# Splitting the weights of the output projection and the feed-forward ahead, as a background stream, and storing the parts through GpSimd's DMA queue

## The chip, the cores and the metric

The kernel runs on one core of a Trainium2 chip. The metric is the time of one execution on the device, in microseconds. A core has five engines, each of which works through its own instructions in order: PE (matrix multiply, with PEld for loading its weights), DVE (vector), ACT (scalar), POOL (GpSimd) and SP (here it only issues DMAs). A DMA is issued by an engine's queue, and an issue that has to wait for a semaphore holds up everything behind it on that engine. In what follows SPq is SP's queue.

## The reference, cut to what matters

One layer of a hybrid encoder for 2048 prompt frames with 16 meta tokens ahead, and 64 sample frames. Rows go through an RMS norm and one wide projection, whose columns feed three groups of mixers; their outputs go through the output projection and a gated feed-forward.

```python
def _trunk(x, states, segs, p):                       # DEPTH = 1
    m, ns = _mixer(_rmsnorm(x, p['norm1_w'][l]), ...)
    x = x + m
    x = x + _swiglu(_rmsnorm(x, p['norm2_w'][l]), p['w_gate'][l], p['w_up'][l], p['w_down'][l])
    return _rmsnorm(x, p['final_norm_w']), ...

def _mixer(h, ...):
    proj = einsum('btd,dn->btn', h, p['w_in'][l])     # 1024 x 5384
    ...                                               # Mamba-2 SSD, RWKV-7, HGRN2
    out = einsum('btm,md->btd', y, p['w_out'][l])     # 1536 x 1024

def _swiglu(h, wg, wu, wd):                           # 1024 x 2816, twice, and 2816 x 1024
    return (silu(h @ wg) * (h @ wu)) @ wd
```

All inputs are float32. The three mixers are causal and carry a state, so frames go through them in order.

## The kernel before, in words

**Tiles.** Rows are cut into 17 tiles (tile 0: the 64 sample frames and the 16 meta tokens; tiles 1 to 16: 128 prompt frames each). The projection (`projection`) works on three blocks of rows, each of two chunks of three tiles (`BLOCKS`, `CHUNKS`). Its results go to DRAM scratch. The mixers read them back a tile at a time: `rw_mixer` (RWKV) is one stream of work, `hs_mixer` (HGRN and SSD) a second. The output projection and feed-forward (class `Ffn`: `out`, `ffn`, `down`, `rest`) work on five groups of tiles: three of three tiles (`EARLY`), then two of four (`LATE`).

**Weights in two parts.** Every float32 weight is multiplied as two parts, hi (rounded) and lo (the rest), and every row operand too, so that a product takes three matmuls. Weights come in units of 128x512. `load_unit` (L205 to 221) gives a unit's two parts in one tile `w` of the ring, of which there are WB = 5. The first time a unit is used, it is loaded as float32 into a tile `raw` (L215, of which there are RB = 3), ACT rounds it into the hi half of `w` (L216), POOL (three units of four) or DVE (the fourth) subtracts to give the lo half (L218), and SP stores the whole `w` of 512 KB to DRAM (L220). Each later use of that unit is one load of 512 KB (L212). There are 84 units of the input projection, and 156 units of the output projection (24), gate and up (88) and down (44).

So the 84 units are split in block 0 of the projection, while PE uses them, and the 156 units in the first pass of the output projection and feed-forward (tiles 0 to 2, `fs[0]`), while PE uses them.

**Streams.** `flow` runs the main work (first the projection, then the early groups). Each piece of it yields its cost, which moves a clock `now` on; a `Stream` whose own clock `t` is not beyond `now` gets the next piece of its work put into the program, and its clock moves on by that piece's cost times the stream's scale (RWX, HSX). So the mixers are written into the program between the matmuls of the main work. A scheduler that knows estimated durations then sets the order on each engine; where a tile of a ring is used again, the instruction that writes it waits until the former use has ended. `drain` steps all streams until given tiles have gone through the mixers.

**DMA queues.** Almost all DMAs are issued by SP. POOL issues the mixers' results (`y`, L750, L879, L972), the final states and part of the output.

Of the kernel before, what the change touches and what calls it, by code (L numbers as in the profile page):

```python
# [9 lines left out]
F32 = mybir.dt.float32  # L10
# [9 lines left out]
P = 128  # L20
# [19 lines left out]
CF = 2  # L40
GKS = 1
GLO = 3
URB = 6
RWX, HSX, HSD = 1.05, 1.0, 6.0
COL = 1 / 2360
AHEAD = 4
KOUT = [8, 9, 10, 11, 0, 1, 2, 3, 4, 5, 6, 7]
# [29 lines left out]
def body(tc, A, O, blocks=None, supers=None, dbg=None):  # L77
# [14 lines left out]
    def mk(p, shape, dt=F32, tag=None, bufs=None):  # L92
        uid[0] += 1
        kw = {} if bufs is None else {"bufs": bufs}
        return p.tile(list(shape), dt, tag=tag, name=f"{tag}_{uid[0]}", **kw)
# [110 lines left out]
    def load_unit(src):  # L206

        key = str(src)
        wt = mk(ring, [P, 2, 512], F32, tag="w", bufs=WB)
        hi, lo = wt[:, 0].bitcast(F32R), wt[:, 1].bitcast(F32R)  # L210
        if key in split:
            nc.sync.dma_start(wt, split[key])  # L212
            return hi, lo
        raw = mk(ring, [P, 512], tag="raw", bufs=RB)
        nc.sync.dma_start(raw, src)  # L215
        S.activation(hi, raw, AF.Copy)  # L216
        units[0] += 1
        (G if units[0] % 4 < GLO else V).tensor_tensor(lo, raw, wt[:, 0], SUB)  # L218
        d = split[key] = dram.tile([P, 2, 512], F32, tag=f"w{units[0]}", name=f"w{units[0]}")
        nc.sync.dma_start(d, wt)  # L220
        return hi, lo

    def inv_rms(p, ss, n, w, mult, eps):
        V.tensor_scalar(ss[:n], ss[:n], mult, eps, MUL, ADD)  # L224
# [840 lines left out]
    nc.sync.dma_start(Shg, A["hg_s0"])  # L1065
    nc.sync.dma_start(Sss, A["ss_s0"])

    def projection():
        for si, sb in enumerate(sbs):
            tiles = sum([CHUNKS[ci] for ci in sb], [])  # L1070

            head = (lambda ci: chunk[ci].v()) if si else (lambda ci: g1([ci], "rw", A["w_rw"], range(HEAD)))
            yield from head(sb[0])
            for ci in sb[1:]:
                if si == 0:
                    chunk[ci].fetch()
                yield from chunk[ci].load()
                yield from head(ci)
            yield from g1(sb, "rw", A["w_rw"], range(0 if si else HEAD, 14))
            ready["rw"] += tiles  # L1080
            banks = yield from gemm_dt(A["w_dt"], [(chunk[ci].hT, chunk[ci].N) for ci in sb])
            dts = [chunk[ci].dt(ps) for ci, ps in zip(sb, banks)]

            def after(ct):
                if ct in DSTEP:
                    for d in dts:
                        next(d, None)
            after(-1)
            yield from g1(sb, "hg", A["w_hg"], range(12), after)
            yield from g1(sb, "xb", A["w_xb"], range(8))  # L1090
            nxt = sbs[si + 1] if si + 1 < len(sbs) else []
            if nxt:
                chunk[nxt[0]].fetch()
            if si == 0:
                for ci in sb:
                    yield from chunk[ci].v()
            for i, ci in enumerate(sb):
                tail = chunk[ci].z()
                yield from weave(tail, chunk[nxt[0]].load()) if nxt and i else tail
            if nxt:  # L1100
                for ci in nxt[1:]:
                    chunk[ci].fetch()
            ready["hs"] += tiles
            if si == 0:
                nc.sync.dma_start(O["s_shift"], scarry)
                nc.sync.dma_start(O["s_conv"], sccarry)
            if si == len(sbs) - 1:
                nc.sync.dma_start(O["p_shift"], carry)
                nc.sync.dma_start(O["p_conv"], ccarry)
# [328 lines left out]
```

## Time and profile before

| what | value |
|---|---|
| median of 3 runs | 3614.21 us (3605.3 to 3619.85) |
| profiled execution, its own time | 3607.34 us |
| its span in the profile | 3605.6 us, 60375 instructions |
| PE / PEld busy | 96% / 84% of the span |
| DVE / ACT / POOL busy | 54% / 30% / 17% of the span |
| mean granted PE clock | 0.982 |
| moved by DMA | 825.75 MB, 229 GB/s over the span |

The stages, from the span's start, in us: block 0 of the projection to about 400, blocks 1 and 2 to 1389, then the first pass of output projection and feed-forward to 1874, the second to 2322, the third (its last part beside group 3's output projection), and from 2618 on the last groups, with no mixers left. Busy is the time in which an engine has an instruction under way. For PE it is a poor measure of the work done, since a matmul that takes longer at a lower granted clock is busy all the same.

### The profile page before, as it was taken

Reading aid. Unit: us, or ns where it says so; the run is one execution under the profiler, and the core shown is the slowest. Engines: PE = TensorE matmul, PEld = TensorE weight load, DVE = VectorE, ACT = ScalarE, POOL = GpSimd, SP = SyncE. Lnnn points to the kernel's source line nnn. Section 1 sums busy time; section 2 is a strip of 40 time slices with the busy share of each in tenths; the row PEclk is TensorE's granted clock in tenths of the full one; section 3 lists DMA queues with packets and bytes.
Section 4 is the critical chain, followed back from the end, with each engine's and each line's share of the span. In section 5 each row is a group of like instructions: output and inputs, shape, how many; then the busy total and the mean of one; then the engine's idle time right before and its main releaser. Section 6 shows DMA issues by size and latency. Waiting matters only on the chain.

```text
span 3605.6 us, 60375 instructions
## 1 busy us (share of the span) xinstructions
PE 3462.9 (96%) x23056; PEld 3033.5 (84%) x23056; DVE 1960.2 (54%) x4612; ACT 1067.1 (30%) x2380; POOL 610.1 (17%) x811
## 2 busy tenths in 40 slices
PE   7999999999999998989889999999999999999998
PEld 7998689989799996778778988879989888878887
DVE  3358546558756676787776676666423322232223
ACT  4445333344433444434343122331110101010001
POOL 3325202102111123345431010110000000000000
PEclk9999999999999999899999999999999999999999
DMA  8776865555666668788897776766867755556554
GB/s 308 233 228 219 291 209 177 159 171 176 239 213 183 198 205 303 263 282 311 299 312 258 229 226 228 249 227 220 287 218 245 263 191 188 181 204 208 193 194 170
DMA packets 396106, 825.75 MB, mean 229 GB/s; under 512 B 107985, under 2 KB 195545, under 8 KB 393769
## 3 DMA queue, kind: packets, MB, share of 16 engines
q1 hardware_dynamic: 389912, 802.75, 67.1%
q0 software_dynamic: 5904, 19.14, 1.4%
q8 instruction: 182, 2.98, 0.3%
q14 instruction: 108, 0.88, 0.1%
HBM read 617.71 MB, written 204.04 MB: 228 GB/s over the span
## 4 chain that ended last, share of the span: by engine, by line
PE 43%; DMA 6%; DVE 6%; SPq 1%; issue 1%; POOL 1%; ACT 1%; DVEq 0%; POOLq 0%; ACTq 0%
PE g L106 32%; PE d L106 6%; PE c L106 2%; PE h L106 2%; DMA w<-w 1%; DMA raw<-in_w_down 1%; DMA raw<-in_w_up 1%; DVE acc L1264 0%; DMA b4k<-psc 0%; DMA y<-hin 0%; DVE Xp L637 0%; DMA hin<-hg 0%; DVE tp L636 0%; POOL w L218 0%; DMA psc<-L 0%
## 5 line engine op out<-in xcount | busy, mean ns | idle before, releaser
L106 PE MATMUL g<-h2hi,w 128*128 128x384 f32 (+2 forms) x3520 | 986.1, 357 | 12.9 <-DMA w<-w 4.6
L106 PE MATMUL g<-hhi,w 128*128 128x384 f32 (+3 forms) x3312 | 835.5, 330 | 11.6 <-DMA w<-w 4.4
L106 PEld LDWEIGHTS g<-h2hi,w 128*128 128x128 f32 x3520 | 639.2, 189 | 81.9 <-ACT w L216 6.9
L106 PE MATMUL g<-h2lo,w 128*128 128x384 f32 (+2 forms) x1760 | 625.4, 355 | 0.0
L106 PEld LDWEIGHTS g<-hhi,w 128*128 128x128 f32 (+1 forms) x3312 | 581.6, 188 | 26.7 <-POOL w L218 4.1
L106 PE MATMUL g<-hlo,w 128*128 128x384 f32 (+3 forms) x1680 | 550.7, 328 | 0.0
L106 PEld LDWEIGHTS g<-h2lo,w 128*128 128x128 f32 x1760 | 332.3, 189 | 32.7 <-DVE h2lo L251 0.2
L106 PEld LDWEIGHTS g<-hlo,w 128*128 128x128 f32 (+1 forms) x1680 | 314.8, 187 | 5.7
L218 POOL TENSOR_TENSOR w<-raw,w 128x512 fp32r<-128x512 f32 x180 | 247.8, 1379 | 336.6 <-ACT w L216 292.4
L106 PE MATMUL g<-w,mhi 128*128 128x512 f32 x792 | 264.0, 410 | 13.0 <-ACT w L216 4.4
L1222 DVE TENSOR_TENSOR w2k<-g,w2k 128x512 f32<-128x512 f32 x44 | 30.4, 692 | 363.1 <-PE g L106 357.0
L226 POOL TENSOR_TENSOR rs<-ss,half 128x1 f32<-128x1 f32 (+2 forms) x51 | 31.0, 609 | 1132.8 <-DVE ss L224 1119.8
L106 PE MATMUL d<-w,mhi 128*128 128x512 f32 x704 | 216.7, 389 | 0.0
L216 ACT ACTIVATE w<-raw 128x512 fp32r<-128x512 f32 x240 | 149.5, 627 | 197.0 <-PE g L106 52.0
L106 PEld LDWEIGHTS g<-w,mhi 128*128 128x128 f32 x792 | 148.9, 193 | 49.4 <-ACT w L216 5.9
L106 PE MATMUL g<-w,hhi 128*128 128x512 f32 (+1 forms) x544 | 179.2, 410 | 10.9 <-DMA w<-w 7.0
L1264 DVE TENSOR_TENSOR acc<-d,acc 128x512 f32<-128x512 f32 x176 | 121.6, 692 | 119.6 <-PE d L106 118.2
L106 PE MATMUL g<-w,h2hi 128*128 128x512 f32 x544 | 175.8, 402 | 10.4 <-DMA w<-w 6.8
L636 DVE TENSOR_TENSOR tp<-Xp,b4k 128x60 f32<-128x60 f32 (+24 forms) x527 | 132.1, 251 | 66.6 <-DMA b4k<-psc 54.0
L106 PE MATMUL g<-w,mlo 128*128 128x512 f32 x396 | 158.6, 401 | 0.0
L106 PEld LDWEIGHTS d<-w,mhi 128*128 128x128 f32 x704 | 132.2, 188 | 27.9
L1264 DVE TENSOR_TENSOR acc<-g,acc 128x512 f32<-128x512 f32 (+1 forms) x198 | 132.4, 683 | 41.1 <-PE g L106 41.0
(359 smaller groups left out, 5299.5 us busy)
## 6 DMA issues: line engine op xcount, KB each, us to landing
w<-w SPq DMA_DIRECT2D x1088, 512.0 KB, 4.1
hin<-hg SPq DMA_DIRECT2D x16, 1280.0 KB, 6.2
rin<-rw SPq DMA_DIRECT2D x16, 896.0 KB, 6.1
yr<-y SPq DMA_DIRECT2D x51, 256.0 KB, 4.7
hg<-stage SPq DMA_DIRECT2D x64, 192.0 KB, 3.0
sin<-ss SPq DMA_DIRECT2D x16, 768.0 KB, 6.1
raw<-in_w_gate SPq DMA_DIRECT2D x44, 256.0 KB, 4.3
raw<-in_w_up SPq DMA_DIRECT2D x44, 256.0 KB, 4.3
```

Source lines behind the costliest of these rows:

```text
L106: return T.matmul(out, lhsT, rhs, start=start, stop=stop)
L216: S.activation(hi, raw, AF.Copy)
L218: (G if units[0] % 4 < GLO else V).tensor_tensor(lo, raw, wt[:, 0], SUB)
L226: G.tensor_tensor(rs[:n], ss[:n], half[:n, 0:w], ALU.pow)
L636: V.tensor_tensor(tv, _bc(Xp[:, 0:m, q], 2, w), _bc(Up[:, q, q + 1:32], 1, m), MUL)
L1222: V.tensor_tensor(sg[:, NS], pu[:, NS], sg[:, NS], MUL)
L1264: V.tensor_tensor(self.acc[:n, i, cs], ps[:n], self.acc[:n, i, cs], ADD)
```

## The change

**A fourth stream.** After block 0 of the projection a third stream beside the two mixers is started, `split_ahead(later())`. `later` lists the sources of all 156 later units in the order of their first use. For each source `split_ahead` loads it into a tile `raw` (SP), ACT rounds it into a second tile of the same ring, POOL subtracts in place (`raw` becomes the lo part), and POOL issues two stores of 256 KB each, one of the hi and one of the lo part, to the unit's place in DRAM. Each unit counts as cost 1.0, and the scale is SPX = 5.0, so a unit is put into the program at every 5 units of `now`. Where `load_unit` later finds the source in `split`, it only loads the 512 KB. The ring `raw` still has three tiles, of which a unit of the stream takes two. DVE has no part in these units.

**The other queue.** The store in `load_unit` (block 0's units) is issued by POOL in place of SP.

```diff
+SPX = 5.0
...
-        nc.sync.dma_start(d, wt)
+        G.dma_start(d, wt)
         return hi, lo
+
+    def split_ahead(srcs):
+
+        for src in srcs:
+            if str(src) in split:
+                continue
+            raw, hi = (mk(ring, [P, 512], tag="raw", bufs=RB) for _ in range(2))
+            nc.sync.dma_start(raw, src)
+            S.activation(hi.bitcast(F32R), raw, AF.Copy)
+            G.tensor_tensor(raw.bitcast(F32R), raw, hi, SUB)
+            units[0] += 1
+            d = split[str(src)] = dram.tile([P, 2, 512], F32, tag=f"w{units[0]}", name=f"w{units[0]}")
+            for i, part in enumerate((hi, raw)):
+                G.dma_start(d[:, i], part)
+            yield 1.0
...
+    def later():
+
+        yield from (A["w_out"][hf, k] for hf in range(2) for k in KOUT)
+        for f in range(NFF):
+            yield from (A[n][f][:, k0 * P:(k0 + 4) * P] for n in ("w_gate", "w_up") for k0 in range(0, KD, 4))
+            if f % CF == CF - 1:
+                yield from (A["w_down"][g * P:(g + 1) * P, hf * 512:hf * 512 + 512]
+                            for hf in range(2) for g in range(f + 1 - CF, f + 1))
...
             if si == 0:
+                streams.append(Stream(split_ahead(later()), SPX))
                 nc.sync.dma_start(O["s_shift"], scarry)
```

**What moves in the order.** The scheduler's order was read for both kernels; a line number of the changed kernel is 1 higher in `load_unit` and 16 higher behind the new function `split_ahead`. Three places matter.

On SP, in the first pass of the feed-forward (gate and up of tiles 0 to 2). Before, each unit is a load of `raw` and, in between, the store of an earlier unit:

```order
L215 DMA raw_18323<-in_w_gate 128x512
L220 DMA w_18262<-w_18257 128x1024
L215 DMA raw_18352<-in_w_gate 128x512
L220 DMA w_18269<-w_18264 128x1024
L215 DMA raw_18377<-in_w_up 128x512
L220 DMA w_18327<-w_18322 128x1024
L215 DMA raw_18426<-in_w_up 128x512
L220 DMA w_18356<-w_18351 128x1024
```

In the changed kernel the units of that pass are loads of both parts (L213), and the stream's last sources (L230) stand between them:

```order
L213 DMA w_17980<-w_10003 128x1024
L230 DMA raw_19473<-in_w_gate 128x512
L213 DMA w_18003<-w_10137 128x1024
L213 DMA w_18017<-w_10207 128x1024
L213 DMA w_18052<-w_10321 128x1024
L213 DMA w_18074<-w_10461 128x1024
L213 DMA w_18097<-w_10554 128x1024
L230 DMA raw_19538<-in_w_up 128x512
```

No store is left on SP there. Of the stream's 156 units, 131 stand on ACT ahead of the first operation of that pass, and the other 25 in it.

On POOL, in a later block of the projection, around an update of the RWKV state (`Srw`; `carry` and `graw` belong to the projection's epilogue, `us` to the HGRN mixer). Before:

```order
L687 TENSOR_TENSOR Srw_6935<-Srw_5583,pc_6219 128x512
L348 COPY carry<-graw_6481 128x1
L346 COPY graw_6489<-carry 128x1
L346 COPY graw_6603<-carry 128x1
L348 COPY carry<-graw_6489 128x1
L782 TENSOR_TENSOR us_6514<-us_6513,us_6514 128x256
```

And in the changed kernel (L703 is the state's update, L232 and L236 are the stream's subtraction and stores):

```order
L232 TENSOR_TENSOR raw_7232<-raw_7232,raw_7233 128x512
L236 DMA w_7237<-raw_7233 128x512
L236 DMA w_7237<-raw_7232 128x512
L703 TENSOR_TENSOR Srw_7111<-Srw_5639,pc_6331 128x512
L364 COPY carry<-graw_6747 128x1
L362 COPY graw_6755<-carry 128x1
L362 COPY graw_6858<-carry 128x1
L232 TENSOR_TENSOR raw_7328<-raw_7328,raw_7329 128x512
L236 DMA w_7333<-raw_7329 128x512
L236 DMA w_7333<-raw_7328 128x512
```

A subtraction and two stores now stand between the mixers' and the projection's small operations; in these rows four of those lie between two such groups. The subtraction waits for ACT's rounding, and the store of the lo part for the subtraction.

On POOL in block 0. Before:

```order
L218 TENSOR_TENSOR w_1245<-raw_1246,w_1245 128x512
L218 TENSOR_TENSOR w_1276<-raw_1277,w_1276 128x512
L342 COPY scarry<-graw_1137 128x1
L343 COPY carry<-graw_1137 128x1
L346 COPY graw_1150<-carry 128x1
```

In the changed kernel:

```order
L221 DMA w_1335<-w_1330 128x1024
L219 TENSOR_TENSOR w_1361<-raw_1362,w_1361 128x512
L221 DMA w_1366<-w_1361 128x1024
L358 COPY scarry<-graw_1222 128x1
L359 COPY carry<-graw_1222 128x1
```

The stores of whole units have come from SP to POOL, and with them those of units whose lo part DVE makes.

## The prediction

> **What bounds the kernel now.** I read the page first, then the stages in windows, then what PE waited for in two of them.
>
> ```profile
> PE 3462.9 (96%) x23056; PEld 3033.5 (84%) x23056; DVE 1960.2 (54%) x4612; ACT 1067.1 (30%) x2380; POOL 610.1 (17%) x811
> ```
>
> PE is busy nearly always, so PE bounds the kernel on average, and time can only be won where PE is late or runs at a lower clock. The stages (busy us and instructions of each engine, then the granted clock, the share of the DMA engines, GB/s):
>
> ```profile
> core 0: us, PE busy (x) PEld busy (x) DVE busy (x) ACT busy (x) POOL busy (x), PEclk, DMA share, GB/s
> 100.00:400.00 300.00, 290.51 (x2007) 267.99 (x2006) 174.74 (x419) 133.15 (x290) 101.06 (x147) 0.99 0.73 234
> 400.00:1389.00 989.00, 960.80 (x7736) 870.48 (x7734) 638.35 (x1717) 395.67 (x899) 170.50 (x295) 0.98 0.64 202
> 1389.00:1874.00 485.00, 438.12 (x3199) 371.88 (x3199) 364.75 (x763) 201.55 (x436) 203.98 (x158) 0.94 0.84 293
> 1874.00:2322.00 448.00, 437.63 (x3277) 386.39 (x3276) 307.55 (x793) 122.91 (x296) 51.37 (x60) 1.00 0.71 239
> ```
>
> The row 1389 to 1874 stands out: PE busy 90% at clock 0.94, DMA at 293 GB/s, POOL four times as busy as in the pass after it. It is the pass that splits the 156 later units. What PE waited for in it (first five rows), and the longest wait of the next pass (last row):
>
> ```profile
> PE g L106 <- ACT w L216: 10.7, 5, 4.4
> PE h L106 <- ACT us L916: 6.3, 3, 2.8
> PE g L106 <- DVE w L218: 5.4, 4, 2.3
> PE h L106 <- DVE Sss L951: 4.9, 2, 3.1
> ...
> PE g L106 <- POOL w L218: 2.1, 4, 0.8
> ...
> PE g L106 <- DMA w<-w: 4.1, 3, 1.6
> ```
>
> Waits for a unit's parts come first, and mixers (`h`) that are late come next. In the next pass neither is there.
>
> **The gain in the first pass.** The two passes hold the same work but for the width of the gate and up matmuls. They start with the output projection:
>
> ```profile
> 1389.26 1.22 PE L106 MATMUL g<-w,y3hi 128*128 128x512 f32 x2
> ...
> 1873.68 0.70 PE L106 MATMUL g<-w,y3hi 128*128 128x512 f32 x2
> ...
> 2321.73 0.70 PE L106 MATMUL g<-w,y3hi 128*128 128x512 f32 x2
> ```
>
> So the first takes 484.4 us and the second 448.0, though the first has the narrower matmuls (one row of the first, then three of the second, by shape):
>
> ```profile
> L106 PE MATMUL g<-h2hi,w 128*128 128x320 f32 x704 | 168.7, 321 | 7.5 <-ACT w L216 4.2 <-DVE acc L1264 1.2 <-DVE w L218 1.1
> ...
> L106 PE MATMUL g<-h2hi,w 128*128 128x384 f32 x704 | 187.1, 340 | 0.8 <-ACT h2hi L250 0.8
> L106 PE MATMUL g<-h2lo,w 128*128 128x384 f32 x352 | 119.0, 339 | 0.0
> L106 PE MATMUL g<-w,mhi 128*128 128x512 f32 x264 | 84.4, 398 | 1.6 <-DMA w<-w 1.6
> ```
>
> The clock was full there, so 398 - 340 = 58 ns for 128 columns, 29 ns for 64, times 704 + 352 = 1056 matmuls: 31 us. A first pass as undisturbed as the second would take 448.0 - 31 = 417, so splitting costs 67 us now. The change takes 131 of the 156 units out of this pass; the other 25 are split beside it, ahead of their use. I take the share: 67 x 131/156 = **56 us won**. The most is 67. The least is what PE waited for the parts themselves, 10.7 + 5.4 + 2.1 = 18 us, if clock and mixers do not recover. Transfers do not take the gain back: a unit in this pass cost 256 KB in and 512 KB out, and now 512 KB in.
>
> **The price in the projection.** The 131 units now fall into the 989 us of blocks 1 and 2, 7.55 us apart. Each brings the following (ACT's rounding, POOL's subtraction, and for the issue of a store of 256 KB on POOL the nearest row, a mixer's result):
>
> ```profile
> L216 ACT ACTIVATE w<-raw x240: 612/631/698, 18.1 to 1863.3; 128x512 fp32r<-128x512 f32 x120
> L218 POOL TENSOR_TENSOR w<-raw,w x180: 1261/1295/2722, 18.8 to 1864.0; 128x512 fp32r<-128x512 f32 x180
> L750 POOL DMA_DIRECT2D y<-ur x17: 539/614/653, 285.4 to 2546.0; - x17
> ```
>
> ACT: 131 x 0.63 = 83 us on 396 of 989. POOL: 131 x (1.30 + 2 x 0.61) = 330 us on 170, together 500 of 989. Neither is full. DMA: 131 x 0.79 MB = 103 MB on 202 GB/s x 989 us = 200 MB, so 306 GB/s, a little above the 293 of the pass that splits now. PE itself gets nothing to do; what it can lose is time in which ACT or POOL, in order, wait on the stream and mixers or PSUM evictions come late. Bounds: nothing, since in 100 to 400 PE works beside units split at the spot and is as busy (290.5 of 300, clock 0.99) as in 400 to 1389 (97%, 0.98); and the same loss per unit as now, 56 us, if all of the disturbance moves along. Half of what PE waits for now, by the five rows, is a unit's parts, and that wait can't move, since no matmul of the projection needs them; units also come at less than half the rate (484/156 = 3.1 us now). So I take a third, **18 us lost**, nearer the row of 100 to 400.
>
> **The other queue in block 0.** SP's waits for the parts, over the whole run:
>
> ```profile
> SPq L220 <- POOL w L218: 222.2, 117, 7.8
> SPq L220 <- DVE w L218: 65.0, 29, 6.4
> ```
>
> Behind them stand the next loads. But in 100 to 400 PE is idle for 9.5 us only, so no more can be won; POOL gets 84 x 0.61 = 51 us on a queue that is two thirds idle there, and where DVE makes the lo part POOL now waits for it, ahead of its small copies for the projection. I take **2 us won**, bounds 9.5 won and as much lost. The Trainium skill's page "DMA: Bandwidth & Descriptors", section "Issuing engines are not separate DMA queues", says that all queues run on the same 16 engines and another issuer saves only the time of issuing. By that rule nothing is won here but a wait at the head of SP's queue, and the sum would be 2 us higher.
>
> **Work at no cost.** The stores' landing holds up nobody in the first pass, since the loads of those units come hundreds of us later. RWKV's last tile moves later against the feed-forward; behind the mixers' last matmul there are still 188 feed-forward matmuls ahead of the group that needs their memory (278 before), which covers a few us of lateness; without that cover it would cost these few us once.
>
> **Sum.** 3607.3 (the profiled execution; span 3605.6) - 56 + 18 - 2 = 3567. The profiled execution lies 6.9 us below the median of the runs, so against that median: **3574 us**, 1.1% faster.
>
> **Rival 1, slower: the stream's three tiles set the pace.** The stream takes two of the ring's three `raw` tiles for a unit, so ACT's rounding of a unit writes the tile from which the lo part before it was stored, and waits until that store has landed. ACT works in order, and behind it stand PSUM evictions. Landing of POOL's stores (KB, us from issue to landing; the first row from 400 to 1389, the other two from 1389 to 1874):
>
> ```profile
> y<-ur POOLq DMA_DIRECT2D x8, 256.0 KB, 3.4
> ...
> y<-hin POOLq DMA_DIRECT2D x4, 256.0 KB, 4.7
> ...
> y<-ur POOLq DMA_DIRECT2D x3, 256.0 KB, 4.4
> ```
>
> A unit's period is 0.63 + 1.30 + 0.61 (the hi part's issue) + 3.4 = 5.9 us, and 7.2 with 4.7. That is within 7.55, and speaks for my forecast, if barely. The rival decides from a landing of 5.0 us on. The longest landing of these stores was 7.0:
>
> ```profile
> DMA to landing us min/median/max: 2.3/4.0/7.0
> ```
>
> With 5.8, about midway between 4.7 and 7.0, the period is 8.3 us, 131 x 8.34 = 1093 us in place of 989: 104 lost in place of 18. Time: 3607.3 - 56 + 104 - 2 + 6.9 = 3660, slower by 1.3%. Chance 0.17.
>
> **Rival 2, no change: the transfers of the projection don't fit.** If 293 GB/s is the most that this mix of sizes reaches, the 303 MB take 1034 us in place of 989: 45 lost, 3607.3 - 56 + 45 - 2 + 6.9 = 3601. For it: the projection's many small packets. Against it: at 293 GB/s the share was 0.84, not 1. Chance 0.14.
>
> **Rival 3: stores on POOL are held up by DVE.** If POOL could issue only while DVE is idle, 0.61 us would become 0.61/(1 - 638/989) = 1.72 us, the period 0.63 + 1.30 + 1.72 + 3.4 + 1.1 = 8.15, 131 x 8.15 = 1068, 79 lost: 3635, slower by 0.6%. Against it: in 17 issues none took over 0.653 us, with DVE 65% busy. Chance 0.03. The Trainium skill's page "SBUF — State Buffer" states such a lock (section "SBUF: two separate sides": while DVE runs in a mode with two ports, GpSimd can't write descriptors) and gives 3100 ns for a transfer of 620 (section "A bandwidth-pool intuition that's wrong (but worth ruling out)"). By its figure, an estimate, two stores would add 5 us to each period and several hundred us to the whole; the 17 issues do not agree, as far as they go.
>
> **Rival 4: the change does not do what it says**, the pass still splits its own units. Then 3614 - 2 = 3612, chance 0.02. The instructions' order, with 131 units ahead of the pass, speaks against it.
>
> **How the numbers follow.** The likeliest case has 0.64 and a range of its own from 3614 - 67 - 9.5 = 3538 to 3614 - 18 - 2 = 3594. About 0.5%, 18 us, is what a measurement of this kernel can tell from no change, so faster is below 3596 and slower above 3632. Faster: 0.64. Same: rivals 2 and 4, 0.16. Slower: rivals 1 and 3, 0.20. The range that should hold the time 8 times in 10 starts at 3540 and reaches through rival 2 into the near part of rivals 1 and 3, to 3640.
>
> **What would show it.** Right: the first pass, from its first matmul of the output projection to that of the second, takes about 428 us at a clock near 1.00, with no waits of PE for L216 or L218 in it; blocks 1 and 2 take some 1007 us in place of 989; PE's busy share there stays above 95%. For rival 1: ACT's longest waits in 400 to 1389 are for landings of the lo part's store ahead of L231, and L231's starts lie 8 us or more apart. For rival 2: a DMA share above 0.95 there, and PE waiting for `w<-w`. For rival 3: stores of L236 of over 1 us on POOL. I am wrong as a whole if blocks 1 and 2 grow by over 50 us, or if the first pass stays above 460 us.

## The result, and the profile after

The changed kernel takes 3662.4 us in the median of four runs (3659.6 to 3665.1), the kernel before 3612.2 us beside it (3605.3 to 3619.9). The ratio is 1.0141, with a 95% interval of 1.0121 to 1.0160: slower, where 3574 us and 1.1% faster had been predicted. The profiled execution has a span of 3657.8 us.

First the engines of the changed kernel, from the page of the profile:

```profile
PE 3480.4 (95%) x23056; PEld 3049.4 (83%) x23056; DVE 1958.7 (54%) x4573; ACT 1062.4 (29%) x2383; POOL 859.6 (24%) x1246
```

PE does the same 23056 matmuls, in 17 us more of busy time, and its span is 52 us longer. The stages, cut at the first matmul of the output projection of each pass:

```profile
1482.99 1.22 PE L107 MATMUL g<-w,y3hi 128*128 128x512 f32 x2
...
1904.99 0.71 PE L107 MATMUL g<-w,y3hi 128*128 128x512 f32 x2
```

The windows of the changed kernel at these places, with the columns of the prediction's rows: blocks 1 and 2, the three passes of tiles with mixers beside them, and the rest.

```profile
400.00:1483.00 1083.00, 983.91 (x7558) 883.26 (x7556) 678.45 (x1670) 450.29 (x1014) 467.80 (x679) 0.96 0.83 273
1483.00:1905.00 422.00, 408.06 (x3132) 355.33 (x3131) 288.10 (x706) 126.83 (x297) 103.61 (x121) 0.98 0.87 295
1905.00:2368.00 463.00, 449.05 (x3433) 398.70 (x3431) 313.72 (x790) 124.96 (x308) 54.49 (x60) 0.99 0.70 231
2368.00:2669.00 301.00, 289.57 (x2089) 254.68 (x2088) 188.61 (x469) 73.39 (x171) 35.34 (x41) 0.98 0.73 246
2669.00:3657.00 988.00, 976.93 (x4374) 811.50 (x4372) 276.74 (x443) 107.42 (x213) 13.86 (x25) 1.00 0.62 206
```

The first pass fell from 484.4 to 422 us, and its clock rose from 0.94 to 0.98: the gain is there. Blocks 1 and 2 grew from 989 to 1083 us. That is 94 us, and two things make it up. PE's busy time rose from 960.8 to 983.9 us at a clock of 0.96 in place of 0.98, for 178 matmuls fewer. And PE's idle time (length less busy time) rose from 28 to 99 us. The 178 are in the main RWKV's matmuls, which came too late for this stage: one of RWKV's tiles fewer has its result stored in it (7 in place of 8). The first pass has 67 matmuls fewer than before as well. They show up later: the second pass has 156 more than before and is 15 us longer, the third 50 more and 5 us longer (most of the remaining 39 of these 245 came earlier, before 400 us). The rest kept its length (987 before, 988 now). Together 94 - 62 + 15 + 5 = 52 us, the difference of the spans.

What PE waited for in blocks 1 and 2 of the changed kernel (us in total, times, longest):

```profile
PE c L107 <- ACT ur L535: 12.5, 5, 4.4
PE c L107 <- DVE ur L667: 11.0, 4, 5.2
PE g L107 <- DMA w<-w: 9.1, 6, 2.2
PE c L639 <- DVE b4k L623: 5.9, 2, 3.9
PE h L107 <- DVE hin L844: 5.7, 4, 1.7
```

No row is long. Four of these five, the longest, are the mixers' matmuls (`c` of RWKV, `h` of the other two), which wait for what ACT and DVE prepare; only 9 us are for weights. In the first pass PE no longer waits for ACT, DVE or POOL to make a unit's parts. Its two longest waits there:

```profile
PE c L107 <- DVE b4k L712: 4.4, 1, 4.4
PE g L107 <- DMA w<-w: 2.5, 4, 1.4
```

The stream itself ran as slowly as rival 1 had it. ACT, SP's queue and POOL each waited on it, in blocks 1 and 2 (one row from each engine's list):

```profile
ACT raw L231 <- DMA w<-raw: 169.1, 58, 7.7
...
SPq L230 <- DMA w<-raw: 229.1, 83, 8.2
...
POOL raw L232 <- ACT raw L231: 395.0, 114, 12.6
```

A rounding waits for the landing of a store (169 us), the next unit's load waits for one at the head of SP's queue (229 us), and POOL stands 395 us before subtractions whose rounding is late. 130 units in 1083 us are 8.3 us a unit, where 7.55 was planned.

Last, the transfers beside the stream. Issue to landing (KB, median us) in blocks 1 and 2, before:

```profile
w<-w SPq DMA_DIRECT2D x216, 512.0 KB, 4.1
hin<-hg SPq DMA_DIRECT2D x7, 1280.0 KB, 6.4
rin<-rw SPq DMA_DIRECT2D x8, 896.0 KB, 5.9
b4k<-psc SPq DMA_DIRECT2D x28, 128.0 KB, 3.8
psc<-L SPq DMA_DIRECT2D x28, 32.0 KB, 2.0
```

and in the changed kernel:

```profile
w<-w SPq DMA_DIRECT2D x212, 512.0 KB, 5.2
hin<-hg SPq DMA_DIRECT2D x7, 1280.0 KB, 8.9
rin<-rw SPq DMA_DIRECT2D x7, 896.0 KB, 7.7
b4k<-psc SPq DMA_DIRECT2D x28, 128.0 KB, 5.0
psc<-L SPq DMA_DIRECT2D x28, 32.0 KB, 4.1
```

The weights' transfers (`w<-w`) are prefetched: they land 1.1 us later, and PE waits 9 us for them in all. The other four are mixers' transfers, each of which stands in a chain of steps, and their medians are 1.2 to 2.5 us longer, though the DMA engines were busy for 0.83 of the time and no more.

So the question for the experiments was: what makes up the price in blocks 1 and 2? Candidates were the ring of three tiles (rival 1), the transfers (rival 2), the order in which ACT and POOL work, and a mere change in the order of all instructions.

### The profile page after: what moved, and what is told of

It reads as the page before. It is cut to its first block, busy times and chain, and to the rows that moved or that the text cites. A ratio compares the mean times of both kernels' runs of the same rounds, so it can differ in the third digit from the quotient of the medians.

```text
span 3657.8 us, 60805 instructions
## 1 busy us (share of the span) xinstructions
PE 3480.4 (95%) x23056; PEld 3049.4 (83%) x23056; DVE 1958.7 (54%) x4573; ACT 1062.4 (29%) x2383; POOL 859.6 (24%) x1246
## 4 chain that ended last, share of the span: by engine, by line
PE 59%; DMA 18%; DVE 9%; issue 5%; POOL 4%; ACT 3%; SPq 1%; POOLq 0%; ACTq 0%; DVEq 0%
PE g L107 45%; DMA w<-raw 7%; PE d L107 6%; PE c L107 3%; DMA w<-w 3%; PE h L107 2%; POOL raw L232 2%; DMA hin<-hg 1%; DVE gcv L430 1%; DMA raw<-in_w_gate 1%; DMA raw<-in_w_down 1%; DMA raw<-in_w_up 1%; DMA y<-hin 1%; ACT raw L231 1%; DVE tp L652 1%
## 5 line engine op out<-in xcount | busy, mean ns | idle before, releaser
L107 PE MATMUL g<-hhi,w 128*128 128x384 f32 (+3 forms) x3312 | 844.5, 333 | 14.9 <-DMA w<-w 5.8
L107 PEld LDWEIGHTS g<-hhi,w 128*128 128x128 f32 (+1 forms) x3312 | 590.2, 191 | 29.1 <-issue 6.5
L232 POOL TENSOR_TENSOR raw<-raw,raw 128x512 fp32r<-128x512 f32 x156 | 213.4, 1368 | 480.3 <-ACT raw L231 479.5
L107 PE MATMUL g<-w,mhi 128*128 128x512 f32 x792 | 252.3, 398 | 2.0 <-DMA w<-w 1.7
L231 ACT ACTIVATE raw<-raw 128x512 fp32r<-128x512 f32 x156 | 98.2, 630 | 321.6 <-DMA w<-raw 198.2
L236 POOL DMA_DIRECT2D w<-raw x312 | 172.6, 554 | 5.1 <-issue 4.8
```

The source lines that it names most:

```text
L107: return T.matmul(out, lhsT, rhs, start=start, stop=stop)
L231: S.activation(hi.bitcast(F32R), raw, AF.Copy)
L232: G.tensor_tensor(raw.bitcast(F32R), raw, hi, SUB)
L236: G.dma_start(d[:, i], part)
```

## The experiments

All times of blocks 1 and 2 below run from 400 us to the first pass's first matmul. Beside the length stands PE's idle time in it, length less busy time, since matmuls that move to a later stage shorten the length, while the idle time counts only the gaps. Where the runs below differ in the number of units that fall into blocks 1 and 2, that number is given. In the edits, `spare[0]` is the constant tile `g2`; `...` stands for lines left out.

**The other queue alone.** The kernel before with the stores of `load_unit` on POOL, no stream:

```diff
-        nc.sync.dma_start(d, wt)
+        G.dma_start(d, wt)
```

> The kernel before, with the stores of load_unit issued by POOL for all 240 units, and no stream. All theories of the stream have the loss elsewhere: block 0 is 0 to 8 us shorter, the first pass of the feed-forward some us shorter too as SP no longer waits for the parts, so 3590 to 3615. If the other queue is itself part of the loss: 3625 or more.

Measured: 3604.1 us, ratio 0.9987 (0.9973 to 1.0001), within what was expected. Blocks 1 and 2 and the first pass:

```profile
400.00:1370.00 970.00, 949.50 (x7694) 862.15 (x7692) 638.12 (x1713) 387.60 (x894) 169.90 (x296) 0.99 0.64 203
1370.00:1850.00 480.00, 430.03 (x3197) 366.19 (x3197) 372.27 (x759) 196.88 (x431) 280.55 (x309) 0.96 0.85 296
```

PE is idle for 20 us in blocks 1 and 2, and the first pass is as long as before. The whole loss belongs to the stream.

**The stream's stores on SP.** The changed kernel, the stores of L236 on SP:

```diff
-                G.dma_start(d[:, i], part)
+                nc.sync.dma_start(d[:, i], part)
```

> As the change, but the stream's two stores of each unit are issued by SP in place of POOL. Theory 1: the ring's waits stay, since the landing through SP takes about as long, and SP now also waits for the subtraction with all loads behind it: 3650 to 3690. Theory 3 (POOL's queue crowded by 312 issues and 173 us of issuing): blocks 1 and 2 fall to some 1020 us, 3590 to 3620. Theory 2: no change, 3650 to 3670.

Measured: 3670.2 us, ratio 1.0180 (1.0160 to 1.0199); blocks 1 and 2 take 1101 us with PE idle for 108 and 145 units in them, the first pass 434. Which queue the stream's stores use is not the cause. The landings of the four mixers' transfers in blocks 1 and 2 of this run:

```profile
hin<-hg SPq DMA_DIRECT2D x7, 1280.0 KB, 8.4
rin<-rw SPq DMA_DIRECT2D x8, 896.0 KB, 5.9
b4k<-psc SPq DMA_DIRECT2D x28, 128.0 KB, 3.9
psc<-L SPq DMA_DIRECT2D x28, 32.0 KB, 2.4
```

Only that of `hin` is over 0.4 us longer than before, and yet the loss is as large as in the changed kernel, by the unit too (0.61 us above the 20 without a stream). So longer landings of these four can't be the whole account.

**A slower stream.** `SPX` 8 in place of 5:

> As the change, with SPX = 8.0 in place of 5.0: some 80 of the units in blocks 1 and 2 of the projection, 12 us apart, the others beside the first pass. Theory 1: a period of 8 us or less no longer sets the pace, blocks 1 and 2 take 1000 to 1020 us, the first pass 430 to 450, the whole 3580 to 3605. Theory 2: the projection's transfers fall from 273 to about 245 GB/s, but those of the first pass rise beyond what it had (295): 3610 to 3640.

Measured: 3669.1 us, ratio 1.0167 (1.0144 to 1.0191).

```profile
400.00:1451.00 1051.00, 971.14 (x7525) 872.41 (x7523) 659.76 (x1667) 432.13 (x967) 391.04 (x581) 0.97 0.79 260
1451.00:1935.00 484.00, 440.82 (x3378) 379.67 (x3375) 340.34 (x787) 159.31 (x368) 154.50 (x170) 0.95 0.76 261
```

98 subtractions fall into blocks 1 and 2 here, and 130 in the changed kernel. Idle time is 80 and 99 us. Over the 20 us without a stream, that is 0.61 us for each unit in both. But the pace on the chip was nearly the same, for the stream's subtractions end long before the stage does (durations, then first and last start):

```profile
L232 POOL TENSOR_TENSOR raw<-raw,raw x98: 1251/1287/2691, 403.0 to 1270.6; 128x512 fp32r<-128x512 f32 x98
```

So a unit came every 8.9 us while the stream ran, against 8.3 in the changed kernel, and the 180 us behind it had no unit. Both theories' ranges were missed (3580 to 3605 and 3610 to 3640), and this run doesn't tell the ring from the rest. And the first pass won nothing, since the units that were left over were split beside it.

**Stores from a tile that never changes.** The changed kernel, both stores reading a constant tile (`g2`), so that no tile of the ring waits for a landing (the stored parts are then not the weights'):

```diff
-            for i, part in enumerate((hi, raw)):
-                G.dma_start(d[:, i], part)
+            for i in range(2):
+                G.dma_start(d[:, i], spare[0])
```

> The stream does all that it does in the change (load, ACT's rounding, POOL's subtraction, two stores of 256 KB issued by POOL), but both stores read one fixed tile that is never written again, so a tile of the raw ring is free as soon as the subtraction is done. The stored parts are therefore not the weights' (this part of the computation is left out). If the three raw tiles set the pace (theory 1): ACT's waits for a store's landing ahead of the rounding (198 us now) are gone, the projection's blocks 1 and 2 fall from 1083 to below 1020 us, the whole to 3565 to 3600. If the transfers' bytes do it (theory 2) or POOL's crowded queue (theory 3): bytes and POOL's work are the same, so blocks 1 and 2 stay above 1060 and the whole at 3640 to 3670.

Measured: 3800.2 us, ratio 1.0546 (1.0520 to 1.0572). This run doesn't answer the question. Stores that depend on nothing were scheduled into block 0: from 100 to 400 us the DMA engines were then busy for 0.95 of the time, and PE did 1342 matmuls in place of 2007. It was done again with the stores kept in place (`ring_free`).

**Bytes alone, and computing alone.** Two streams on top of the other queue, whose results nobody uses; the first pass splits its own units again. The steps are tied to the projection's matmuls in the scheduler's order, without a wait on the chip. (`last[0]` is the last matmul written out.)

```diff
+            ins = [last[0], nc.sync.dma_start(raw, src)]
+            in_turn(ins)
...
+            in_turn([last[0]] + [G.dma_start(d[:, i], spare[0]) for i in range(2)])
```

> The stream only moves bytes: per unit one load of 256 KB and two stores of 256 KB from a tile that never changes, tied in order to the projection's matmuls, with no rounding and no subtraction. The first pass still splits its own units, so it should stay near 484 us in every theory. Left out: nothing of the result; the stored bytes are not used. Blocks 1 and 2 (970 us without the stream, with the stores on the other queue; 1083 in the changed kernel): the theory that the transfers don't fit expects 1060 to 1090, total about 3700. The theories of the ring and of order on POOL and ACT expect 970 to 995, total 3600 to 3630.

```diff
+            in_turn([last[0], S.activation(hi.bitcast(F32R), spare[0], AF.Copy)])
+            G.tensor_tensor(raw.bitcast(F32R), spare[0], hi, SUB)
```

> The stream only computes: per unit one rounding on ACT and one subtraction on POOL, both of a tile that never changes, tied in order to the projection's matmuls, with no load and no store. The first pass still splits its own units. Left out: nothing of the result; what is computed is not used. Blocks 1 and 2: the theory of order on POOL and ACT (mixers' operations behind the stream's) expects 1000 to 1040, total 3635 to 3675; the theories of the ring and of the transfers expect 970 to 985, total about 3605 to 3620.

Measured: 3811.2 us, ratio 1.0531 (1.0513 to 1.0548), and 3782.4 us, ratio 1.0450 (1.0434 to 1.0465). Blocks 1 and 2 and the first pass of the stream of bytes:

```profile
400.00:1476.00 1076.00, 990.21 (x7772) 893.27 (x7768) 652.98 (x1751) 394.54 (x915) 285.41 (x523) 0.94 0.80 268
1476.00:2145.00 669.00, 547.43 (x4103) 454.05 (x4103) 484.44 (x1072) 249.78 (x577) 358.57 (x429) 0.89 0.81 281
```

and of the stream that computes:

```profile
400.00:1438.00 1038.00, 977.06 (x7748) 883.08 (x7746) 705.15 (x1732) 450.98 (x1020) 324.15 (x405) 0.97 0.60 189
```

The totals say little: in both, the first pass takes 670 us, which no theory had; the rest of the stream falls into it and takes tiles of the ring that the pass needs for its own units. Blocks 1 and 2 can be read (113 units of bytes, 114 of computing). Bytes alone make PE idle for 86 us there, with no rounding that could wait for the ring and no subtraction. Computing alone makes it idle for 61. By the length each theory found its own range met, 1076 us in 1060 to 1090 and 1038 in 1000 to 1040; since both lose, neither can be the whole price.

**The ring alone.** `const_store` again, the two stores held behind their subtraction in POOL's order:

```diff
-            G.tensor_tensor(raw.bitcast(F32R), raw, hi, SUB)
+            ins = [G.tensor_tensor(raw.bitcast(F32R), raw, hi, SUB)]
...
-            for i, part in enumerate((hi, raw)):
-                G.dma_start(d[:, i], part)
+            for i in range(2):
+                ins.append(G.dma_start(d[:, i], spare[0]))
+            in_turn(ins)
```

> The changed kernel, its two stores reading a tile that never changes, issued on POOL at the same place behind the subtraction. No rounding can wait for a landing any more; bytes and instructions are the same. Left out: the stored parts are not the weights. Blocks 1 and 2: the ring theory expects about 1000 us, total about 3580. The transfers expect 1080, total 3660. The order on POOL and ACT expects 1040 to 1075 (POOL still waits for a rounding that waits for a load), total 3620 to 3655.

Measured: 3642.5 us, ratio 1.0069 (1.0054 to 1.0084).

```profile
400.00:1460.00 1060.00, 970.68 (x7524) 871.49 (x7523) 701.69 (x1666) 461.90 (x1025) 524.08 (x754) 0.97 0.89 300
```

Without a wait for landings all 156 units fit ahead of the first pass. Blocks 1 and 2 are 23 us shorter than in the changed kernel, PE's idle time is 89 in place of 99, and the whole is 0.7% (26 us by the two ratios) faster, within the range of the theory of order on ACT and POOL. Since 26 units more are split in the stage, the fair measure is the unit: 0.44 us of idle time above the 20 without a stream, in place of 0.61. So the ring is about a quarter of the price, and the rest stays when it is gone.

**A unit's steps spread over its period.** The rounding half a period behind the load, the subtraction a quarter behind the rounding, each tied behind the projection's matmul of that time:

```diff
             nc.sync.dma_start(raw, src)
...
+            yield 0.5
+            in_turn([last[0], S.activation(hi.bitcast(F32R), raw, AF.Copy)])
+            yield 0.25
+            in_turn([last[0], G.tensor_tensor(raw.bitcast(F32R), raw, hi, SUB)])
...
-            yield 1.0
+            yield 0.25
```

> The changed kernel with a unit's steps spread over its period: the load half a period ahead of the rounding, the rounding a quarter ahead of the subtraction and the stores, each tied in order behind the projection's matmul of that time. The ring, the bytes and the instructions are the same. The order on POOL and ACT expects that POOL waits less for ACT, blocks 1 and 2 at 1000 to 1040, total 3580 to 3620. The ring and the transfers expect no change, 1080 and 3660 (the ring even somewhat more, since a store is issued later).

Measured: 3704.1 us, ratio 1.0237 (1.0222 to 1.0253); blocks 1 and 2 take 1092 us with PE idle for 98, and the first pass 492, since only 102 units were split by then. The theory of order, which had 1000 to 1040 us, missed. POOL's waits for ACT's rounding did shrink, from 395 us to 242 (2.4 us a unit in place of 3.0), and PE's idle time didn't. So those waits are not the main part of the price.

**What one step costs, and what a stream of nothing costs.** Four streams of 131 units on top of the other queue, each with one operation: nothing but a tiny memset, the rounding, the subtraction, the load:

```diff
+            in_turn([last[0], G.memset(raw[0:1, 0:1], 0.0)])
...
+            in_turn([last[0], S.activation(raw.bitcast(F32R), spare[0], AF.Copy)])
...
+            in_turn([last[0], G.tensor_tensor(raw.bitcast(F32R), spare[0], spare[0], SUB)])
...
+            in_turn([last[0], nc.sync.dma_start(raw, src)])
```

> A stream of 131 units that does next to nothing: per unit one memset of one number on POOL, tied to the projection's matmuls like the streams of the two runs before. The first pass splits its own units. It asks what a stream costs by the new order of all instructions alone. Nothing of the result is left out. Blocks 1 and 2 (970 us without a stream, and 95 us of them beyond the matmuls' own time): the theory that any new order loses expects 1030 or more; the theories of contention (for ACT, POOL or the transfers) expect 965 to 985, total 3600 to 3625.

> As the null stream, but a unit is ACT's rounding alone (0.63 us, of a tile that never changes). Nothing of the result is left out. If the loss of the stream that only computed (50 to 68 us in blocks 1 and 2) is ACT's, 1010 to 1030; if it is POOL's, 970 to 990, total 3605 to 3625.

> As the null stream, but a unit is POOL's subtraction alone (1.3 us, of a tile that never changes, so that it waits for nothing). Nothing of the result is left out. If POOL's time costs (mixers' operations and copies behind it), 1000 to 1030, total 3640 to 3670; if only its wait for ACT costs, 970 to 990, total 3605 to 3625.

> As the null stream, but a unit is the load of 256 KB alone, a third of a unit's bytes. Nothing of the result is left out. If the transfers cost by their bytes, about a third of the 105 us that the stream of bytes lost against 970, so 1005, total 3640; if the stores on POOL cost and not the bytes, 970 to 985, total 3605 to 3620.

Measured, in this order: 3656.6, 3657.3, 3715.9 and 3693.1 us (ratios 1.0106, 1.0110, 1.0273 and 1.0212, each to within 0.0026); no range of a total was met. 113 or 114 of the units fall into blocks 1 and 2, the others into the first pass. Blocks 1 and 2 beside the stream of nothing:

```profile
400.00:1401.00 1001.00, 960.93 (x7713) 870.90 (x7712) 638.29 (x1718) 386.88 (x891) 169.85 (x403) 0.98 0.61 192
```

beside the rounding alone:

```profile
400.00:1403.00 1003.00, 965.27 (x7717) 874.05 (x7716) 636.72 (x1715) 441.58 (x1001) 166.24 (x290) 0.98 0.61 192
```

beside the subtraction alone:

```profile
400.00:1435.00 1035.00, 973.03 (x7742) 878.33 (x7741) 690.50 (x1727) 387.80 (x906) 292.56 (x404) 0.97 0.60 188
```

and beside the load alone:

```profile
400.00:1419.00 1019.00, 968.52 (x7754) 876.56 (x7752) 645.10 (x1730) 388.52 (x907) 166.16 (x290) 0.97 0.69 221
```

PE's idle time is 40, 38, 62 and 50 us. ACT's rounding adds nothing to the null stream, POOL's subtraction adds 22 (and 34 to the length), the loads, a third of the bytes, add 10 (and 18). DVE, for 9 instructions more, is busy for 690 us beside the subtraction and for 638 beside the null stream. The 22 may be too small for the changed kernel: with one tile for both inputs the subtraction took 1.15 us on average, there 1.37. But the null stream itself was not free, and its first pass took 523 us. Either a new order loses by itself, and then every number here is in doubt, or the null stream did, by taking tiles of the ring.

**Two more streams of nothing.** The memset into a tile of its own, 110 units at the same pace, and 80 units at `SPX` 7:

> As the null stream, 110 units, its memset into a tile of its own, so that it no longer shares the ring with the units that the first pass splits. Nothing of the result is left out. If a new order alone loses, blocks 1 and 2 at 990 or more and the first pass above 500, total 3640 or more. If the null stream lost in the first pass by the ring's tiles, the first pass falls back to about 484 and the total to 3610 to 3625, with blocks 1 and 2 somewhere from 970 to 1000, which is the scatter of orders.

> The same at another pace (80 units, 7 apart in place of 5): a third order. If orders scatter, blocks 1 and 2 fall anywhere from 970 to 1005, not tied to the number of units; if a unit of nothing has a price, the loss is below that of the run before, in the proportion 80 to 110.

Measured: 3607.4 and 3605.0 us, ratios 0.9976 (0.9964 to 0.9988) and 0.9975 (0.9962 to 0.9988). Blocks 1 and 2 with 110 units of nothing:

```profile
400.00:1382.00 982.00, 955.95 (x7722) 867.10 (x7719) 639.90 (x1715) 389.05 (x897) 178.68 (x409) 0.98 0.65 202
```

and with 80:

```profile
400.00:1374.00 974.00, 953.18 (x7704) 865.37 (x7703) 638.15 (x1714) 388.19 (x894) 175.46 (x378) 0.99 0.65 203
```

These equal the kernel with the other queue alone, with first passes of 476 and 480 us. A new order need not lose anything; the scatter of blocks 1 and 2 over such orders is 970 to 982 us, and PE's idle time 20 to 26. What the null stream lost in the first pass fits the shared tiles: there 17 of its units fell among the pass's own, and PE waited 21.5 us for ACT to make the hi parts, against 3.2 beside the 110 units. But the number of units was lowered together with the change of tile, and in blocks 1 and 2, where only three other loads use the ring, the null stream's 40 us against 20 to 26 stay unexplained. The streams with one operation are read against it, since they take the ring's tiles as it does; against the streams of nothing with a tile of their own their prices would be 14 to 19 us higher.

**Bytes without POOL.** The stream of bytes with its stores issued on SP, 120 units:

```diff
-            in_turn([last[0]] + [G.dma_start(d[:, i], spare[0]) for i in range(2)])
+            in_turn([last[0]] + [nc.sync.dma_start(d[:, i], spare[0]) for i in range(2)])
```

> The stream of bytes with its stores issued on SP in place of POOL, 120 units. Nothing of the result is left out. If the bytes cost, blocks 1 and 2 stay at 1060 or more. If the issues on POOL cost (1.1 us a unit in order), 1000 to 1020, near the stream of loads alone (1019).

Measured: 3715.5 us, ratio 1.0276 (1.0253 to 1.0298). 112 units fall into blocks 1 and 2.

```profile
400.00:1468.00 1068.00, 982.10 (x7764) 888.00 (x7762) 647.48 (x1745) 395.73 (x917) 166.72 (x297) 0.95 0.82 269
```

PE is idle for 86 us, as with the stores on POOL. So it is the transfers and not POOL's issues (their bytes and their number were not told apart). Nor is it SP's queue standing before the stream's loads, as it did for 229 us in the changed kernel: before the stream's DMAs it stood for some 32 us here, and for 27 in the stream with its stores on POOL. This stream computes nothing, and yet landings beside it are longer than before, all of these but that of `hin`:

```profile
w<-w SPq DMA_DIRECT2D x208, 512.0 KB, 5.5
hin<-hg SPq DMA_DIRECT2D x8, 1280.0 KB, 6.2
rin<-rw SPq DMA_DIRECT2D x8, 896.0 KB, 6.9
b4k<-psc SPq DMA_DIRECT2D x31, 128.0 KB, 5.4
psc<-L SPq DMA_DIRECT2D x32, 32.0 KB, 4.7
```

**The stream's subtraction on DVE.** The changed kernel, and the result is complete:

```diff
-            G.tensor_tensor(raw.bitcast(F32R), raw, hi, SUB)
+            V.tensor_tensor(raw.bitcast(F32R), raw, hi, SUB)
```

> The changed kernel with the stream's subtraction on DVE (0.69 us by the nearest row) in place of POOL; the result is complete. DVE gets 131 x 0.69 = 90 us more in blocks 1 and 2, but its other instructions should be as short as before (gcv 128x384 at 626 ns, 773 in the changed kernel). If POOL's subtraction costs by slowing DVE, blocks 1 and 2 at 1040 to 1065, total 3620 to 3645. If what counts is DVE's time and its wait for ACT in order, 1085 or more, total 3665 or more.

Measured: 3652.0 us, ratio 1.0097 (1.0075 to 1.0119). The length below is in the range expected for it, the total is above its range (3620 to 3645).

```profile
400.00:1444.00 1044.00, 960.62 (x7414) 867.39 (x7412) 681.11 (x1735) 449.10 (x999) 310.01 (x556) 0.97 0.86 287
```

The length fell by 39 us, and PE's idle time from 99 to 83, with 137 units in place of 130. Part of the 39 is only moved: 144 matmuls fewer than in the changed kernel lie in this stage, the first pass is 6 us longer, the second 8 shorter, and the third, to the same place, 30 longer. By the ratios the whole gained 0.44%, 16 us. POOL's wait for the rounding is still there, now ahead of the stream's stores:

```profile
POOL w L236 <- ACT raw L231: 343.1, 104, 8.9
```

So it was the subtraction on POOL that cost these 16 us, and not POOL's waiting, which is hardly shorter. They were won though DVE has the stream's subtractions as well, and DVE's other instructions became short again; POOL's own time of 1.37 us a unit went as well, and the run doesn't separate the two. The same 72 instructions of the projection's convolution on DVE, in blocks 1 and 2, before:

```profile
L414 DVE SCALAR_TENSOR_TENSOR gcv<-graw,cwh,gcv 128x384 f32<-128x384 f32 x72 | 44.5, 626 | 11.2 <-ACT gcv L412 10.4
```

in the changed kernel:

```profile
L430 DVE SCALAR_TENSOR_TENSOR gcv<-graw,cwh,gcv 128x384 f32<-128x384 f32 x72 | 55.4, 773 | 10.6 <-ACT gcv L428 7.9 <-POOL rs L242 1.9
```

and with the stream's subtraction on DVE:

```profile
L430 DVE SCALAR_TENSOR_TENSOR gcv<-graw,cwh,gcv 128x384 f32<-128x384 f32 x72 | 45.7, 643 | 5.0 <-ACT gcv L428 4.6
```

**A version that is faster than both?** The other queue alone once more, and the same with two of four units' subtractions on POOL in place of three (`GLO` 2):

> The kernel before with the stores of the parts on POOL and no stream, once more. If block 0 gains what its first 400 us showed (7 us more of the matmuls' own time done by then than before), the ratio is 0.998 and its interval ends below 1; if the gain was scatter, the interval holds 1.

> The same with two of four units' subtractions on POOL in place of three. If POOL's subtraction costs by slowing DVE, DVE's accumulation and the mixers come earlier in the first pass, 5 to 15 us are won there and the total is 3590 to 3600; if DVE's own time decides (39 x 0.72 = 28 us more in the pass), the pass stays at 480 or grows, total 3605 to 3620.

Measured: 3611.8 us, ratio 0.9978 (0.9967 to 0.9988), and 3605.4 us, ratio 0.9968 (0.9957 to 0.9978). Both beat the kernel before, by 0.2 to 0.3%, and the changed kernel by far more. The second is not faster than the first beyond the intervals, and its first pass took 481 us: the 5 to 15 us that were expected in that pass are not there. Either what POOL's subtraction costs beside the mixers of blocks 1 and 2 does not carry over to that pass, or DVE's own time cancels it; no run separates these.

## Why the prediction was wrong, point by point

**The gain in the first pass: right.** Predicted was a fall from 484 to 428 us; measured 422. A few us of that are matmuls that moved to the second pass (3132 in place of 3199), so the nearness is partly luck. The clock recovered to 0.98, nearly as assumed, and PE's waits for the making of the parts are gone.

**The price in the projection: this is the step that failed.** 18 us predicted, with 0 and 56 as bounds; 94 measured, and 101 to 113 against the four kernels without a stream's work, which take 970 to 982 us. The mechanism that was named (ACT and POOL wait on the stream in order) exists, 395 us of it on POOL, but isn't the main one. "Half of what PE waits for now" was also loosely read: the five rows give 18 of 29 us, which would have made the term smaller still. And the term's own upper bound of 56 never entered the sum: the range of the likeliest case up to 3594 has a price of nothing in it, and 56 lost would have cancelled the whole gain. Two assumptions led to the small number:

- The row from 100 to 400 us was taken as the nearest: PE there works beside units that are split, and is 97% busy. But that stretch has next to no mixers. One result of RWKV and none of the other two is stored before 400 us, against 23 results in blocks 1 and 2. The matmuls that came late are mixers' matmuls. A row from a stretch without the work that is disturbed can't bound what the disturbance costs.
- "Transfers: 306 GB/s, a little above 293" was weighed only as whether they fit. They needn't fail to fit: at a DMA share of 0.80 and 0.82, transfers alone made PE idle for 86 us, against 20 to 26 without them (40 in the null stream that shared the ring's tiles as they did). In the changed kernel four landings in the mixers' chains lengthened by 1 to 3 us, which suggests how; but with the stores on SP three of the four stayed short and the loss was as large. The runs show that the transfers cost this; they do not show the chain by which they do.

What makes up the price, by PE's idle time in blocks 1 and 2: 112 or 113 units of transfers cost 46 us above the null stream that shared the tiles, 114 of POOL's subtractions 22, ACT's roundings nothing. Taken out of the changed kernel one at a time, the ring returns 10 of its 99 and POOL's subtraction 16; by the unit, the 0.61 us fall to 0.44 without the ring's waits and to 0.46 with the subtraction on DVE. The parts overlap and can't be added. The transfers are the largest single part that was measured alone; no run that can be read took them out of the changed kernel.

**The clock in blocks 1 and 2: not foreseen.** It fell from 0.98 to 0.96, and PE's busy time rose by 23 us. Over all these runs a lower clock goes with more idle time (0.98 or 0.99 up to 40 us idle in blocks 1 and 2, 0.97 from 50 to 62, 0.94 to 0.97 from 80 on). I take this quarter of the 94 us as a consequence of the idle time; that is not shown, since no run separates the two.

**The other queue in block 0: right in sign, small in size.** 2 us predicted within 9.5 either way. Alone it gives ratios of 0.9975 to 0.9987 in four runs, some 5 to 9 us. That block 0 itself is where they are won isn't shown: from 100 to 400 us these four kernels did between 4 matmuls fewer and 24 more than the 2007 of before.

**Work at no cost:** the tail did not change (987 and 988 us). But the second and third passes took 15 and 5 us more, with mixers' matmuls that moved there; the prediction had next to nothing for that (a few us of lateness, taken as covered).

**Rival 1, the ring:** its number came true (3660 us, a period of 8.3 us) and its signs are all in the profile, the waits for the lo part's store ahead of the rounding and the wide spacing. Yet with the ring out of the way 23 of the 94 us came back (a quarter, by length as by the unit's idle time), so the cause is mostly another and the number was met by luck. A rival whose number is met still has to be taken out by an experiment.

**Rival 2, the transfers:** its price was half of what was measured and its test failed to see it. The share stayed at 0.83 (a share above 0.95 was asked for), and PE waited for weights for 9 us. It was the right resource with the wrong picture: the pipe was not full when the loss came. That short chains get longer by it is a picture that fits, not one that is shown.

**Rival 3, stores held up by DVE:** not seen. The stream's 312 stores on POOL:

```profile
L236 POOL DMA_DIRECT2D w<-raw x312: 539/557/631, 401.1 to 1723.5; - x156
```

None took over 0.631 us, with DVE busy for 63% of blocks 1 and 2. If anything the hold-up ran the other way: DVE's instructions were longer beside POOL's subtraction.

**Rival 4:** 131 units were split ahead, as the order said.

## What to carry to other kernels

A background stream that fits into every engine's and the DMA engines' idle share can still cost more than it saves, here beside a foreground of short dependent steps with transfers in them: 0.6 us of PE's idle time a unit, against 0.47 us (62 us over 131 units) that a unit saved later. Price such a stream from a stretch that holds the same foreground, and weigh what the foreground's own transfers lose, not only whether the bandwidth is enough. Check on the chip what an experiment has varied: the "slower stream" was hardly slower while it ran. And a control that does nothing should also touch nothing: the null stream that took tiles of the ring lost 1.1%, the two shorter ones with a tile of their own nothing.

## What the runs showed of the hardware that was not expected

POOL's subtraction of 128x512 lengthened DVE's instructions beside it: the convolution's 128x384 instruction took 626 ns before, 773 in the changed kernel, and 643 when the same subtractions ran on DVE. Beside the subtraction alone it took 654, beside the null stream 627. The Trainium skill's page "SBUF — State Buffer", section "SBUF: two separate sides", says that GpSimd and a DVE instruction with two inputs in SBUF share a pair of ports, and that whichever starts first holds it for its whole length. An estimate by that rule: 130 subtractions of 1.37 us (their mean by the page of the profile) take 178 of 1083 us, so a DVE instruction would meet one 16% of the time and wait 0.7 us on average, 113 ns. The row's 147 ns is of that size, but the agreement doesn't carry over: for the subtraction alone (114 of 1.15 us in 1035) the same estimate gives 72 ns, and the rows differ by 27. So the lengthening is shown; that the rule is its cause is not.

DMA landings could grow well before the engines were full. At a share of 0.64 a 32 KB transfer of a mixer took 2.0 us to land, in the changed kernel at 0.83 it took 4.1, and beside the stream of bytes on SP, at 0.82, 4.7. But the share alone doesn't set it: with the stream's stores on SP, at 0.85, it took 2.4.
